# mLSTM in two chunks of 128 tokens in place of four chunks of 64

## The chip, the cores and the metric

The kernel runs on one core of a Trainium2 chip. The metric is the device time of one execution in microseconds, as the median of several runs. The engines are named as in the profile: PE (TensorE, products), PEld (its loads of weights), DVE (VectorE), ACT (ScalarE), POOL (GpSimd) and SP (SyncE, which issues the loads from memory).

## The reference

Two layers work on 256 tokens of width 1024. Each layer is a half-step FFN (SwiGLU), a mixer, and a second half-step FFN, with RMSNorm around each. The mixer projects its input, runs two groups of heads beside each other, differential attention and mLSTM, and projects both back. The change touches the mLSTM alone: 4 heads, keys of 64, values of 128. The reference works it in chunks of CHUNK = 64 tokens; shortened:

```
b = cumsum(log_f)                     # within a chunk
a = b_last - b + log_i
# the scan over chunks, state C (128 x 64), n (64), m:
m_new = max(bl + m, max(a));  w = exp(a - m_new);  decay = exp(bl + m - m_new)
C_new = decay * C + sum_l w_l v_l k_l^T;   n_new = decay * n + sum_l w_l k_l
# within a chunk, with the state from before it:
D = where(causal, b_j - b_s + log_i_s, -inf);  m = max(b + m_prev, max_s D)
w = exp(D - m) * (q k^T);  decay = exp(b + m_prev - m)
num = w v + decay * (q C_prev);  den = sum_s w + decay * (q n_prev)
h = num / max(|den|, exp(-m))
```

The chunk length does not change what h is, only how the sum over earlier tokens is split between the products within a chunk and the products with the state. The mask of the attention beside it has chunks of 64 of its own, and that stays.

## The kernel before

Weights arrive in pieces of 128 x 2048 (1 MB each). ACT makes of each half a rounded high part (wh, line 285), DVE the rest (wl, line 287), and every large product is three products on PE: wh with the high part of the input, wl with it, and wh with its low part (lines 335 to 337). These products are nearly all of PE's work.

In the mixer the projection runs over five groups of 512 columns, each for two tiles of 128 tokens (t = 0, 1). Its products are cut into 88 numbered steps. The small work of attention and mLSTM is cut into stages (`gate_chain`, `gate_decays`, `weighted_qk`, `scores`, `state`, `numerators` in `normed_ml`, `attend` and so on), and the table AT says ahead of which step each stage is issued. On PE the order of the program holds through the mixer. On the other engines a scheduler orders the instructions by its own estimates, and each engine then works its queue in that order.

PSUM holds a pool `bk` of four banks that the stages take in turn. A stage that takes a bank waits until the stage before it in that bank has been read out. Two banks `pin` hold the running projections; ACT or DVE empties one (`vd`, `vx`, `ra` and `rb`) before PE writes it again.

mLSTM with four chunks of 64, two per tile of tokens:
- `gate_chain` makes the running sums and maxima, starting again every 64 tokens (constants `scan`), and mp, the running maximum ahead of each chunk.
- `gate_decays` makes three rows of 256 exponents in ex: the factor of the state in a token's output, the weight of a token in the state, and the floor of the denominator. The first is rounded to eh.
- `weighted_qk` spreads eh over the rows with a product (L928), turns the other two rows round (L932), turns the keys round (L942), and makes qd (queries times the factor), dcy (the state's decay at the end of each chunk) and kwn (keys times their weights, for both tiles).
- `state(c)` for c = 0, 1, 2 makes the state after chunk c: four products of 64 x 64 weights on 129 columns, the last of which gathers the denominator (L1074), and an update of the state on DVE (L1078, L1081).
- `numerators(t)` sums into two banks: for each of the four heads a product within the tile (L1090, all 128 rows; the mask keeps the chunks apart), and behind it the product with the state: one on 64 rows for t = 0 (L1092, state after chunk 0) and two on 64 rows and 64 columns for t = 1 (L1095, states after chunks 1 and 2).
- `normed_ml` squares (ACT), takes the inverse root (POOL, rs), and scales (DVE, hn), which reads the two banks out.

fp32 products of the program make two records each in the trace.

Of the kernel before, what the change touches and what calls it, by code (L numbers as in the profile page):

```python
# [27 lines left out]
DFF = 2816  # L28
NC_FF = DFF // 256
KT = D // P  # L30
CH = 64
EPS = 1e-6
BIG = -1.0e30
DEFER = 3
AHEAD = 2
AT = (0, 2, 6, 6, 7, 22, 24, 24, 24, 24, 36, 31, 24, 38, 56, 34, 40, 40, 52, 57, 61, 60, 61, 67, 67, 67, 67, 71, 71, 78, 74, 74, 78, 84)
WARM = 6
SCRATCH = 1024
FILL = 896
# [82 lines left out]
class _Trunk:  # L122
# [49 lines left out]
    def constants_mix(self):  # L172
        nc, a = self.nc, self.a
# [3 lines left out]
        for name, shape in C1:  # L177
            n = math.prod(shape)
# [6 lines left out]
        for l in range(L):  # L185
# [27 lines left out]
                                     op=ALU.add)  # L213
# [7 lines left out]
        for t in range(NT):  # L221
            i = nc.scalar.activation(self.md[0:36, t], self.hot[0:36].unsqueeze(2).broadcast_to([36, 4, P]), AF.Copy)
# [5 lines left out]
        self.qd = self.ded.tile([P, 2, S], F32, name="qd")  # L228
# [426 lines left out]
class _Mixer:  # L655


    def __init__(self, tr, pre, l):
        self.tr, self.l = tr, l
        self.xT, self.r = pre  # L660
        self.yT = [[None, None] for _ in range(NT)]
        self.conved = None
        self.rot, self.qkT, self.so, self.C, self.p = [], [], [], [None], {}
# [204 lines left out]
    def gate_chain(self):  # L868
        tr, nc, stt, tt, ptg = self.tr, self.tr.nc, self.stt, self.tt, self.ptg
        gt = tr.t4("gt", (100, 4, S))  # L870
        bc, u, cm, M = (gt[:, i, :] for i in range(4))
# [10 lines left out]
        tt(self.c4(M), self.c4(cm), mp.unsqueeze(2).broadcast_to([100, 4, CH]), op=ALU.max)  # L882
# [23 lines left out]

    def gate_decays(self):

        tr, tt, c4 = self.tr, self.tt, self.c4
        bc, u, M = (v[0:36] for v in (self.bc, self.u, self.M))  # L910
        ex = self.ex = tr.t4("ex", (36, 3, S))
        tt(c4(ex[:, 0, :]), self.mp[0:36].unsqueeze(2).broadcast_to([36, 4, CH]), c4(M), op=ALU.subtract)
# [5 lines left out]
        tr.nc.vector.memset(ex[:, 0, 0:CH], 0.0)  # L918
        eh = self.eh = tr.t2("eh", (36, S), F32R)
        self.act(eh, ex[:, 0, :], AF.Copy)  # L920
        tt(eh[32:36], ex[32:36, 0, :], eh[32:36].bitcast(F32), op=ALU.subtract)

    def weighted_qk(self):

        tr, nc = self.tr, self.tr.nc
        pdb = tr.bank_bk((P, 2, S))
        for pr in range(2):
            self.mm(pdb[:, pr, :], tr.hotp[:, pr, :], self.eh, start=True, stop=True)  # L928
        ptn = tr.bank_bk((P, 2, NT, 4))
        for i in range(2):  # L930
            for t in range(NT):
                self.T(ptn[:, i, t, :], self.ex[0:4, 1 + i, t * P:(t + 1) * P], tr.ident[0:4, 0:4])  # L932
        self.wem = tr.small("wem", (P, 2, NT, 4))
# [5 lines left out]
        self.kwn = []  # L939
        for t in range(NT):  # L940
            for pr in range(2):
                self.T(ptk[:, t, pr, :], self.kT[:, pr, t * P:(t + 1) * P], tr.ident)  # L942
        for t in range(NT):
            kw = tr.t2("kwn", (P, 4, 64))
            self.tt(kw, ptk[:, t].rearrange("p a (h d) -> p (a h) d", h=2),
                    self.wem[:, 0, t, :].unsqueeze(2).broadcast_to([P, 4, 64]), op=ALU.mult)
            self.kwn.append(kw)
# [120 lines left out]
    def state(self, c):  # L1068
        tr, nc, mm, vx, C = self.tr, self.tr.nc, self.mm, self.tr.vx, self.C
        t, rows = c // 2, slice((c % 2) * 64, (c % 2) * 64 + 64)  # L1070
        pd = tr.bank_bk((P, 2, P + 1))
        for pr in range(2):
            for hh in range(2):
                mm(pd[hh * 64:hh * 64 + 64, pr, :], self.kwn[t][rows, 2 * pr + hh, :], vx[rows, t, 2 * pr + hh, :],  # L1074
                   start=True, stop=True)
        Cn = tr.small("C", (P, 2, P + 1), 3)
        if c == 0:
            nc.vector.tensor_copy(Cn, pd)  # L1078
        else:
            for pr in range(2):  # L1080
                self.stt(Cn[:, pr, :], C[c][:, pr, :], self.dcy[:, pr, c:c + 1], pd[:, pr, :], op0=ALU.mult, op1=ALU.add)  # L1081
        C.append(Cn)

    def numerators(self, t):
        tr, mm, vx, C = self.tr, self.mm, self.tr.vx, self.C
        num = [tr.bank_bk((P, 2, P + 1)) for _ in range(2)]
        for pr in range(2):
            for hh in range(2):
                rows, out = slice(hh * 64, hh * 64 + 64), num[hh][:, pr, :]
                mm(out, tr.wt[:, t, pr, hh, :], vx[:, t, 2 * pr + hh, :], start=True, stop=False)  # L1090
                if t == 0:
                    mm(out, tr.qd[rows, pr, 0:P], C[1][rows, pr, :], start=False, stop=True)  # L1092
                else:
                    for c in (2, 3):
                        mm(out[(c - 2) * 64:(c - 1) * 64], tr.qd[rows, pr, c * CH:(c + 1) * CH], C[c][rows, pr, :],  # L1095
                           start=False, stop=True)
# [13 lines left out]
    def normed_ml(self, t):  # L1110

        tr, act, tt = self.tr, self.act, self.tt
        num = self.numerators(t)
        ss = tr.small("ssm", (P, 4))
        dm = tr.small("dm", (P, 4))
        for h in range(4):
            act(tr.junk_tile(P), num[h % 2][:, h // 2, 0:P], AF.Square, scale=2.0 ** -3.5, accum_out=ss[:, h:h + 1])
        for hh in range(2):
            act(dm[:, hh::2], num[hh][:, :, P], AF.Abs)
        tt(dm, dm, self.wem[:, 1, t, :], op=ALU.max)  # L1120
        tt(dm, dm, dm, op=ALU.mult)
        self.stt(ss, dm, EPS, ss, op0=ALU.mult, op1=ALU.add)
        self.ts(ss, ss, 1e-37, 1e37, op0=ALU.max, op1=ALU.min)
# [50 lines left out]
```

## Time and profile before

| | before |
|---|---|
| median of 3 runs | 1004.95 us (1004.37 to 1006.48) |
| profiled execution | 1004.17 us |
| its span | 1002.4 us |
| mean granted TensorE clock | 0.996 |
| PE busy | 987.8 us, 99% of the span |
| DVE busy | 615.6 us, 61% |
| ACT busy | 523.6 us, 52% |
| POOL busy | 57.9 us, 6% |

The span runs from the first to the last instruction of the profiled execution; its own time is 1.77 us more. A row of the timeline gives the start, the time from start to end, the engine and line, what is written from what, the shape, the count, and in brackets the time that the engine stood idle before it and what ended that. Products overlap on PE, so the distance between two starts, not the duration, is what a product costs there. The mixer of the first layer lies about between 205 and 310 us, that of the second between 697 and 803 us.

### The profile page before, as it was taken

What the parts mean: (1) busy time and instruction counts of PE and PEld (TensorE: products, weight loads), DVE (VectorE), ACT (ScalarE), POOL (GpSimd) and SP (SyncE); (2) the same over time, 40 slices, a digit from 0 to 9 for tenths busy, and PEclk for the clock granted to TensorE, in tenths of its full rate; (3) what the DMA queues carried; (4) which work ended last, traced back from release to release, by engine and by line L of the source; (5) the groups of instructions that cost most, each with busy time, mean ns of one, the idle gap of its engine ahead of it and who ended that gap; (6) DMA issues with size and microseconds to landing.
All of it is one profiled execution on the core that took longest, in us unless ns stands there. A gap on an engine that the chain in (4) does not pass through costs nothing.

```text
span 1002.4 us, 12193 instructions
## 1 busy us (share of the span) xinstructions
PE 987.8 (99%) x4701; PEld 807.1 (81%) x4701; DVE 615.6 (61%) x867; ACT 523.6 (52%) x853; POOL 57.9 (6%) x59
## 2 busy tenths in 40 slices
PE   8999999999999999999999999999999999999997
PEld 5888888887788888888888888888877888888885
DVE  6755554589766755555485645456988586455542
ACT  6645444466755654445274544445768465454431
POOL 2000000014010000000000000001220100000000
PEclk9999999999999999999999999999999999999999
DMA  7954545335352745455346455543554247554511
GB/s 281 353 204 161 200 174 196 124 126 192 129 205 84 278 164 210 168 217 195 134 185 257 157 193 196 199 149 114 188 170 141 112 158 284 180 198 168 205 48 43
DMA packets 26809, 178.86 MB, mean 178 GB/s; under 512 B 2970, under 2 KB 3354, under 8 KB 6014
## 3 DMA queue, kind: packets, MB, share of 16 engines
q1 hardware_dynamic: 26750, 178.07, 48.5%
q8 instruction: 37, 0.61, 0.2%
q14 instruction: 22, 0.18, 0.1%
HBM read 177.01 MB, written 1.05 MB: 178 GB/s over the span
## 4 chain that ended last, share of the span: by engine, by line
PE 93%; DVE 4%; ACT 1%; DMA 1%; issue 0%; SPq 0%; DVEq 0%; POOLq 0%; ACTq 0%
PE pin L335 19%; PE pin L337 19%; PE pin L336 19%; PE bk L335 10%; PE bk L337 10%; PE bk L336 10%; PE ptr L466 2%; DVE wl L287 2%; DVE conv L810 1%; PE ptr L354 1%; ACT p L250 1%; PE ptr L778 1%; DMA wr<-in_w_dram 1%; PE bk L1090 1%; PE bk L1045 1%; ACT wh L285 0%
## 5 line engine op out<-in xcount | busy, mean ns | idle before, releaser
L287 DVE TENSOR_TENSOR wl<-wr,wh 128x1024 fp32r<-128x1024 f32 (+1 forms) x332 | 397.3, 1218 | 227.0 <-ACT wh L285 217.3
L285 ACT ACTIVATE wh<-wr 128x1024 fp32r<-128x1024 f32 (+1 forms) x332 | 340.5, 1045 | 203.0 <-PE pin L337 110.4
L335 PE MATMUL pin<-wh,th 128*128 128x512 f32 x880 | 349.2, 397 | 0.6 <-DVE rb L976 0.6
L337 PE MATMUL pin<-wh,tl 128*128 128x512 f32 x880 | 343.9, 391 | 0.0
L336 PE MATMUL pin<-wl,th 128*128 128x512 f32 x880 | 343.4, 390 | 0.0
L337 PEld LDWEIGHTS pin<-wh,tl 128*128 128x128 f32 x880 | 165.2, 188 | 35.0
L335 PEld LDWEIGHTS pin<-wh,th 128*128 128x128 f32 x880 | 165.3, 188 | 34.5 <-PE ptr L778 1.0
L336 PEld LDWEIGHTS pin<-wl,th 128*128 128x128 f32 x880 | 165.5, 188 | 32.4
L335 PE MATMUL bk<-wh,hh 128*128 128x512 f32 x352 | 140.0, 398 | 0.0
L337 PE MATMUL bk<-wh,hl 128*128 128x512 f32 x352 | 137.9, 393 | 0.0
L336 PE MATMUL bk<-wl,hh 128*128 128x512 f32 x352 | 137.6, 391 | 0.0
L469 ACT ACTIVATE hh<-ptr 128x256 fp32r<-128x256 f32 x88 | 33.2, 378 | 96.8 <-PE ptr L466 79.3
L250 ACT ACTIVATE sil<-pin,rs 128x256 f32<-128x256 f32 x86 | 40.6, 472 | 72.3 <-PE pin L337 69.0
L337 PEld LDWEIGHTS bk<-wh,hl 128*128 128x128 f32 x352 | 66.1, 188 | 13.7
L336 PEld LDWEIGHTS bk<-wl,hh 128*128 128x128 f32 x352 | 66.2, 188 | 12.7
L335 PEld LDWEIGHTS bk<-wh,hh 128*128 128x128 f32 x352 | 66.1, 188 | 12.8
L470 DVE TENSOR_TENSOR hl<-ptr,hh 128x256 fp32r<-128x256 f32 x88 | 37.0, 421 | 55.3 <-ACT hh L469 52.5
L343 POOL TENSOR_TENSOR rs<-s,c_half 128x1 f32<-128x1 f32 x24 | 18.0, 753 | 780.7 <-DVE s L383 771.4
L459 DVE SCALAR_TENSOR_TENSOR h<-pin,rs,sil 128x256 f32<-128x256 f32 x86 | 41.2, 479 | 30.3 <-ACT sil L250 30.3
L466 PEld LDWEIGHTS ptr<-c,h 128*128 128x128 f32 x176 | 24.7, 140 | 11.5
L400 DVE TENSOR_TENSOR tmp<-bk,gpost 128x512 f32<-128x512 f32 x24 | 16.3, 689 | 28.5 <-ACT junk L397 28.5
L466 PE MATMUL ptr<-c,h 128*128 128x128 f32 x176 | 33.4, 271 | 0.0
(169 smaller groups left out, 615.8 us busy)
## 6 DMA issues: line engine op xcount, KB each, us to landing
wr<-in_w_dram SPq DMA_DIRECT2D x162, 1024.0 KB, 4.8
gpost<-in_gpost_dram SPq DMA_DIRECT2D x6, 512.0 KB, 6.5
wr<-in_w_dram SPq DMA_DIRECT2D x3, 512.0 KB, 8.6
x<-in_x_dram SPq DMA_DIRECT2D x4, 256.0 KB, 7.0
out_dram<-x SPq DMA_DIRECT2D x4, 256.0 KB, 2.0
wr<-in_w_dram SPq DMA_DIRECT2D x2, 256.0 KB, 4.5
lamv<-in_lam_dram SPq DMA_DIRECT2D x1, 256.0 KB, 3.3
c<-in_c_dram SPq DMA_DIRECT2D x1, 222.0 KB, 6.7
```

What stands on the lines that cost most here:

```text
L250: i = self.nc.scalar.activation(*args, **kw)
L285: ia = nc.scalar.activation(hi[:, cs], raw[:, j, cs], AF.Copy)
L287: iv = nc.vector.tensor_tensor(lo[:, cs], raw[:, j, cs], hi[:, cs].bitcast(F32), op=ALU.subtract)
L335: mm(ps, xh, wh, start=start, stop=False)
L336: mm(ps, xh, wl, start=False, stop=False)
L337: mm(ps, xl, wh, start=False, stop=stop)
L343: self.nc.gpsimd.tensor_tensor(r, ss, self.half[:, :width], op=ALU.pow)
L400: nc.vector.tensor_tensor(tmp[hf], po[hf], g[:, hf * 512:hf * 512 + 512], op=ALU.mult)
L459: nc.vector.scalar_tensor_tensor(h, pin[:, 256:512], r, sil, op0=ALU.mult, op1=ALU.mult)
L466: nc.tensor.transpose(ptr[:, k, :], h[:, k * P:(k + 1) * P], self.ident)
L469: nc.scalar.activation(hh, ptr, AF.Copy)
L470: nc.vector.tensor_tensor(hl, ptr, hh.bitcast(F32), op=ALU.subtract)
```

## The change

The chunk length CH becomes 128, the length of a tile. There are two chunks, and the one state that is needed is that after the first tile. The first tile has no state before it, so its numerators have no product with a state at all. In the second tile the four products with the state stand behind all four products within the tile. The mask, the sums and maxima follow CH. ex has two rows in place of three (one row holds the weights of the first tile and the factors of the second), eh, qd and kwn are for one tile, dcy and the updates of the state go. AT loses two entries, those of two of the three `state` stages. The diff, with the helper c4 and signatures cut:

```diff
-CH = 64
+CH = P
@@ gate_chain
-        mp = self.mp = tr.small("mp", (100, 4))
+        mp = self.mp = tr.small("mp", (100, NT))
         nc.vector.memset(mp[:, 0:1], 0.0)
-        nc.vector.tensor_tensor_scan(mp[:, 1:4], self.c4(cm)[:, 0:3, CH - 1], self.c4(bc)[:, 0:3, CH - 1], 0.0,
-                                     op0=ALU.max, op1=ALU.add)
+        stt(mp[:, 1:2], cm[:, CH - 1:CH], 0.0, bc[:, CH - 1:CH], op0=ALU.max, op1=ALU.add)
...
@@ gate_decays
-        ex = self.ex = tr.t4("ex", (36, 3, S))
-        tt(c4(ex[:, 0, :]), self.mp[0:36].unsqueeze(2).broadcast_to([36, 4, CH]), c4(M), op=ALU.subtract)
-        tt(c4(ex[:, 1, :]), c4(u), c4(M)[:, :, CH - 1:CH].broadcast_to([36, 4, CH]), op=ALU.subtract)
-        self.stt(ex[:, 2, :], bc, -1.0, M, op0=ALU.mult, op1=ALU.subtract)
+        ex = self.ex = tr.t4("ex", (36, 2, S))
+        tt(ex[:, 0, 0:CH], u[:, 0:CH], M[:, CH - 1:CH].broadcast_to([36, CH]), op=ALU.subtract)
+        tt(ex[:, 0, CH:S], self.mp[0:36, 1:2].broadcast_to([36, CH]), M[:, CH:S], op=ALU.subtract)
+        self.stt(ex[:, 1, :], bc, -1.0, M, op0=ALU.mult, op1=ALU.subtract)
...
-        tr.nc.vector.memset(ex[:, 0, 0:CH], 0.0)
-        eh = self.eh = tr.t2("eh", (36, S), F32R)
-        self.act(eh, ex[:, 0, :], AF.Copy)
-        tt(eh[32:36], ex[32:36, 0, :], eh[32:36].bitcast(F32), op=ALU.subtract)
+        eh = self.eh = tr.t2("eh", (36, CH), F32R)
+        self.act(eh, ex[:, 0, CH:S], AF.Copy)
+        tt(eh[32:36], ex[32:36, 0, CH:S], eh[32:36].bitcast(F32), op=ALU.subtract)
@@ weighted_qk
-        pdb = tr.bank_bk((P, 2, S))
+        pdb = tr.bank_bk((P, 2, CH))
         for pr in range(2):
             self.mm(pdb[:, pr, :], tr.hotp[:, pr, :], self.eh, start=True, stop=True)
...
-        self.stt(tr.qd, self.q, 0.125, pdb, op0=ALU.mult, op1=ALU.mult)
-        self.dcy = tr.small("dcy", (P, 2, 4))
-        nc.vector.tensor_copy(self.dcy, pdb.rearrange("p a (c j) -> p a c j", c=4)[:, :, :, CH - 1])
-        ptk = tr.bank_bk((P, NT, 2, P))
...
+        self.stt(tr.qd, self.q[:, :, CH:S], 0.125, pdb, op0=ALU.mult, op1=ALU.mult)
+        ptk = tr.bank_bk((P, 2, P))
+        for pr in range(2):
+            self.T(ptk[:, pr, :], self.kT[:, pr, 0:P], tr.ident)
...
@@ state
+        pd = tr.bank_bk((P, 2, P + 1))
+        for pr in range(2):
+            for hh in range(2):
+                self.mm(pd[hh * 64:hh * 64 + 64, pr, :], self.kwn[:, 2 * pr + hh, :], tr.vx[:, 0, 2 * pr + hh, :],
+                        start=True, stop=True)
+        self.C = tr.small("C", (P, 2, P + 1))
+        tr.nc.vector.tensor_copy(self.C, pd)
@@ numerators
         for pr in range(2):
             for hh in range(2):
...
+                mm(num[hh][:, pr, :], tr.wt[:, t, pr, hh, :], tr.vx[:, t, 2 * pr + hh, :],
+                   start=pr == 0, stop=t == 0, skip_group_check=True)
+        if t:
+            for pr in range(2):
+                for hh in range(2):
+                    rows = slice(hh * 64, hh * 64 + 64)
+                    mm(num[hh][:, pr, :], tr.qd[rows, pr, :], self.C[rows, pr, :], start=False, stop=True,
+                       skip_group_check=True)
```

What it moves in the queues is seen at three places of the first layer. Lines shift by the edit: L1037 becomes L1022, L1052 L1037, L1055 L1040, L1127 L1108, L1120 to L1123 become L1101 to L1104. The first place is PE's queue at the state and the numerators of the first tile; L1037 (L1022) are transposes of attention that stand between. Before:

```order
L1074 MATMUL bk_2388<-vx,kwn_2155 64x129 x4
L1074 MATMUL bk_2395<-vx,kwn_2155 64x129 x4
L1037 MATMUL ptr_2406<-c_96,p_2339 128x128 x2
L1037 MATMUL ptr_2406<-c_96,p_2340 128x128 x2
L1090 MATMUL bk_2414<-vx,wt 128x129
L1092 MATMUL bk_2414<-C_2393,qd 128x129
L1090 MATMUL bk_2415<-vx,wt 128x129
L1092 MATMUL bk_2415<-C_2393,qd 128x129
```

With the change:

```order
L1059 MATMUL bk_2380<-vx,kwn_2149 64x129 x4
L1022 MATMUL ptr_2390<-c_96,p_2331 128x128 x2
L1022 MATMUL ptr_2390<-c_96,p_2332 128x128 x2
L1070 MATMUL bk_2398<-vx,wt 128x129
L1070 MATMUL bk_2399<-vx,wt 128x129
L1070 MATMUL bk_2398<-vx,wt 128x129
L1070 MATMUL bk_2399<-vx,wt 128x129
```

Before, four more rows like the last four follow, and twelve large products later a third L1074 x4; both are gone, and the products with the state between the others too. The second place is PE's queue at the numerators of the second tile. Before:

```order
L1090 MATMUL bk_2560<-vx,wt 128x129
L1095 MATMUL bk_2560<-C_2400,qd 64x129
L1095 MATMUL bk_2560<-C_2468,qd 64x129
L1090 MATMUL bk_2561<-vx,wt 128x129
L1095 MATMUL bk_2561<-C_2400,qd 64x129
L1095 MATMUL bk_2561<-C_2468,qd 64x129
```

and the same six once more. With the change these are all:

```order
L1070 MATMUL bk_2532<-vx,wt 128x129
L1070 MATMUL bk_2533<-vx,wt 128x129
L1070 MATMUL bk_2532<-vx,wt 128x129
L1070 MATMUL bk_2533<-vx,wt 128x129
L1076 MATMUL bk_2532<-C_2385,qd 128x129
L1076 MATMUL bk_2533<-C_2385,qd 128x129
L1076 MATMUL bk_2532<-C_2385,qd 128x129
L1076 MATMUL bk_2533<-C_2385,qd 128x129
```

The four products with the state now stand together behind the four within the tile. With two banks fewer taken by `state`, these two banks are now those that numerators(0) had taken. The third place is DVE's queue behind the first tile's denominators, where hn reads the first numerators out; ssa and y belong to `attend`. Before:

```order
L1123 TENSOR_SCALAR ssm_2424<-ssm_2424 128x4
L1127 TENSOR_TENSOR hn_2442<-bk_2414,rs_299_2440 128x2x128
L1127 TENSOR_TENSOR hn_2442<-bk_2415,rs_299_2440 128x2x128
L287 TENSOR_TENSOR wl_0_2663<-wr_2661,wh_0_2664 128x1024
L1052 SCALAR_TENSOR_TENSOR ssa_2503<-l_313_2512,ssa_2503 128x4
```

With the change:

```order
L1104 TENSOR_SCALAR ssm_2404<-ssm_2404 128x4
L287 TENSOR_TENSOR wl_0_2631<-wr_2629,wh_0_2632 128x1024
L1037 SCALAR_TENSOR_TENSOR ssa_2475<-l_307_2484,ssa_2475 128x4
L1108 TENSOR_TENSOR hn_2422<-bk_2398,rs_295_2420 128x2x128
L1108 TENSOR_TENSOR hn_2422<-bk_2399,rs_295_2420 128x2x128
L1040 TENSOR_TENSOR y_2489<-bk_2470,rs_308_2487 128x512
```

hn now stands behind a cast of weights and behind ssa. The queues of POOL and SP keep their order, and ACT's changes only behind the squares of `attend`, where two casts of weights now come after all eight squares.

More of the change, by code (lines that the diff above doesn't have):

```diff
@@ L35 @@
 AHEAD = 2
-AT = (0, 2, 6, 6, 7, 22, 24, 24, 24, 24, 36, 31, 24, 38, 56, 34, 40, 40, 52, 57, 61, 60, 61, 67, 67, 67, 67, 71, 71, 78, 74, 74, 78, 84)
+AT = (0, 2, 6, 6, 7, 22, 24, 24, 24, 24, 36, 31, 24, 38, 56, 34, 40, 40, 52, 57, 61, 60, 61, 67, 67, 67, 71, 78, 74, 74, 78, 84)
 WARM = 6
@@ L227, in constants_mix @@
         self.qk = self.ded.tile([P, 4, S], F32, name="qk")
-        self.qd = self.ded.tile([P, 2, S], F32, name="qd")
+        self.qd = self.ded.tile([P, 2, CH], F32, name="qd")
         self.vx = self.ded.tile([P, NT, 4, P + 1], F32, name="vx")
@@ L662, in __init__ @@
         self.conved = None
-        self.rot, self.qkT, self.so, self.C, self.p = [], [], [], [None], {}
+        self.rot, self.qkT, self.so, self.p = [], [], [], {}
         self.aT, self.lsum, self.hn, self.y = [None] * NT, [None] * NT, [None] * NT, [None] * NT
@@ L751, in stages @@
             lambda: self.scores(1, 2),
-            lambda: self.state(0),
-            lambda: self.state(1),
+            self.state,
             lambda: self.combine(1, 0),
             lambda: self.normed_ml(0),
-            lambda: self.state(2),
             lambda: self.combine(1, 2),
@@ L876, in gate_chain @@
         nc.vector.tensor_tensor_scan(cm, tr.scan[:, 1, :], u, 0.0, op0=ALU.add, op1=ALU.max)
-        mp = self.mp = tr.small("mp", (100, 4))
+        mp = self.mp = tr.small("mp", (100, NT))
         nc.vector.memset(mp[:, 0:1], 0.0)
-        nc.vector.tensor_tensor_scan(mp[:, 1:4], self.c4(cm)[:, 0:3, CH - 1], self.c4(bc)[:, 0:3, CH - 1], 0.0,
-                                     op0=ALU.max, op1=ALU.add)
-        tt(self.c4(M), self.c4(cm), mp.unsqueeze(2).broadcast_to([100, 4, CH]), op=ALU.max)
+        stt(mp[:, 1:2], cm[:, CH - 1:CH], 0.0, bc[:, CH - 1:CH], op0=ALU.max, op1=ALU.add)
+        tt(M.rearrange("p (c j) -> p c j", c=NT), cm.rearrange("p (c j) -> p c j", c=NT),
+           mp.unsqueeze(2).broadcast_to([100, NT, CH]), op=ALU.max)
         mh = tr.t2("mh", (100, S), F32R)
@@ L907, in gate_decays @@
     def gate_decays(self):
-        tr, tt, c4 = self.tr, self.tt, self.c4
+        tr, tt = self.tr, self.tt
         bc, u, M = (v[0:36] for v in (self.bc, self.u, self.M))
-        ex = self.ex = tr.t4("ex", (36, 3, S))
-        tt(c4(ex[:, 0, :]), self.mp[0:36].unsqueeze(2).broadcast_to([36, 4, CH]), c4(M), op=ALU.subtract)
-        tt(c4(ex[:, 1, :]), c4(u), c4(M)[:, :, CH - 1:CH].broadcast_to([36, 4, CH]), op=ALU.subtract)
-        self.stt(ex[:, 2, :], bc, -1.0, M, op0=ALU.mult, op1=ALU.subtract)
+        ex = self.ex = tr.t4("ex", (36, 2, S))
@@ L923, in weighted_qk @@
+        self.act(eh, ex[:, 0, CH:S], AF.Copy)
+        tt(eh[32:36], ex[32:36, 0, CH:S], eh[32:36].bitcast(F32), op=ALU.subtract)
     def weighted_qk(self):
         tr, nc = self.tr, self.tr.nc
-        pdb = tr.bank_bk((P, 2, S))
+        pdb = tr.bank_bk((P, 2, CH))
         for pr in range(2):
             self.mm(pdb[:, pr, :], tr.hotp[:, pr, :], self.eh, start=True, stop=True)
[L929 to L932, printed above, removed]
@@ L933, in weighted_qk @@
-        self.wem = tr.small("wem", (P, 2, NT, 4))
-        nc.vector.tensor_copy(self.wem, ptn)
-        self.stt(tr.qd, self.q, 0.125, pdb, op0=ALU.mult, op1=ALU.mult)
-        self.dcy = tr.small("dcy", (P, 2, 4))
-        nc.vector.tensor_copy(self.dcy, pdb.rearrange("p a (c j) -> p a c j", c=4)[:, :, :, CH - 1])
-        ptk = tr.bank_bk((P, NT, 2, P))
[L939 to L947, printed above, removed]
+        ptn = tr.bank_bk((P, 1 + NT, 4))
+        for n, row in enumerate((self.ex[0:4, 0, 0:P], self.ex[0:4, 1, 0:P], self.ex[0:4, 1, P:S])):
+            self.T(ptn[:, n, :], row, tr.ident[0:4, 0:4])
+        self.wem = tr.small("wem", (P, 1 + NT, 4))
@@ L949, in intra_weights @@
+        nc.vector.tensor_copy(self.wem, ptn)
+        self.stt(tr.qd, self.q[:, :, CH:S], 0.125, pdb, op0=ALU.mult, op1=ALU.mult)
+        ptk = tr.bank_bk((P, 2, P))
+        for pr in range(2):
+            self.T(ptk[:, pr, :], self.kT[:, pr, 0:P], tr.ident)
+        self.kwn = tr.t2("kwn", (P, 4, 64))
+        self.tt(self.kwn, ptk.rearrange("p a (h d) -> p (a h) d", h=2),
+                self.wem[:, 0, :].unsqueeze(2).broadcast_to([P, 4, 64]), op=ALU.mult)
     def intra_weights(self):
@@ L1066, in values_ml, with state @@
                                             AF.Copy, scale=self.r[t])
-    def state(self, c):
-        tr, nc, mm, vx, C = self.tr, self.tr.nc, self.mm, self.tr.vx, self.C
-        t, rows = c // 2, slice((c % 2) * 64, (c % 2) * 64 + 64)
+    def state(self):
+        tr = self.tr
         pd = tr.bank_bk((P, 2, P + 1))
@@ L1073, in state @@
             for hh in range(2):
[L1074 to L1082, printed above, removed]
+                self.mm(pd[hh * 64:hh * 64 + 64, pr, :], self.kwn[:, 2 * pr + hh, :], tr.vx[:, 0, 2 * pr + hh, :],
+                        start=True, stop=True)
+        self.C = tr.small("C", (P, 2, P + 1))
+        tr.nc.vector.tensor_copy(self.C, pd)
     def numerators(self, t):
-        tr, mm, vx, C = self.tr, self.mm, self.tr.vx, self.C
+        tr, mm = self.tr, self.mm
         num = [tr.bank_bk((P, 2, P + 1)) for _ in range(2)]
@@ L1088, in numerators @@
             for hh in range(2):
[L1089 to L1096, printed above, removed]
+                mm(num[hh][:, pr, :], tr.wt[:, t, pr, hh, :], tr.vx[:, t, 2 * pr + hh, :],
[6 more added lines that the diff above has]
+                       skip_group_check=True)
         return num
@@ L1119, in normed_ml @@
             act(dm[:, hh::2], num[hh][:, :, P], AF.Abs)
-        tt(dm, dm, self.wem[:, 1, t, :], op=ALU.max)
+        tt(dm, dm, self.wem[:, 1 + t, :], op=ALU.max)
         tt(dm, dm, dm, op=ALU.mult)
```

3 lines of the change are left out of this document (removed).

## The prediction

> **What bounds the kernel now.** I read the page first: which engine is busy, and whose work the chain of waits runs through.
>
> ```profile
> span 1002.4 us, 12193 instructions
> PE 987.8 (99%) x4701; PEld 807.1 (81%) x4701; DVE 615.6 (61%) x867; ACT 523.6 (52%) x853; POOL 57.9 (6%) x59
> ...
> PE 93%; DVE 4%; ACT 1%; DMA 1%; issue 0%; SPq 0%; DVEq 0%; POOLq 0%; ACTq 0%
> ...
> L287 DVE TENSOR_TENSOR wl<-wr,wh 128x1024 fp32r<-128x1024 f32 (+1 forms) x332 | 397.3, 1218 | 227.0 <-ACT wh L285 217.3
> ```
>
> TensorE is busy for 99% of the span and carries 93% of the chain. Work taken off its queue shortens the run, unless what stands next in the queue is not ready. Its waits in the mixer, for both layers together:
>
> ```profile
> PE bk L928 <- DVE eh L921: 1.5, 2, 0.7
> PE bk L1092 <- DVE C L1078: 0.4, 2, 0.2
> ...
> ACT wh L285 <- DMA wr<-in_w_dram: 19.7, 16, 3.1
> ```
>
> Each count of 2 is once per layer. The layers run alike, so I work out the first and double it. The profiled run took 1004.17 us, 1.77 us beyond its span and 0.78 us under the median of the runs, 1004.95.
>
> **Term A, weights of queries and keys.** TensorE's timeline (start, busy, line, operands, count, idle before):
>
> ```profile
> 242.69 0.50 PE L928 MATMUL bk<-eh,c_hotp 36*128 36x256 f32 x2 [0.74 <-DVE eh L921]
> 243.12 0.41 PE L932 MATMUL bk<-c,ex 4*128 4x4 f32 x4
> 243.46 0.66 PE L942 MATMUL bk<-c,qk 128*128 128x128 f32 x4
> 243.95 0.60 PE L778 MATMUL ptr<-c,ra 128*128 128x128 f32 x4
> 244.35 0.47 PE L335 MATMUL pin<-wh,th 128*128 128x512 f32 x1
> ```
>
> The change halves the columns of L928, drops one of four L932 (0.34/4 = 0.09) and two of four transposes of L942 (0.49/2 = 0.25). The halved columns save between nothing and half of the 0.43 that L928 takes to the next row; I take 0.1, since loading the array is not halved. That is 0.43 us of TensorE, but TensorE waits here for VectorE before and behind:
>
> ```profile
> 230.50 0.41 DVE L912 TENSOR_TENSOR ex<-mp,gt 36x256 f32<-36x256 f32 x1
> 235.11 0.11 DVE L918 MEMSET ex<- 36x64 f32 x1
> 235.15 0.41 DVE L810 SCALAR_TENSOR_TENSOR conv<-xpad,c,conv 128x256 f32<-128x256 f32 x1
> 242.22 0.41 DVE L921 TENSOR_TENSOR eh<-ex,eh 4x256 fp32r<-4x256 f32 x1
> 243.34 0.87 DVE L976 SCALAR_TENSOR_TENSOR rb<-pin,rs,c 128x256 f32<-128x256 f32 x2
> ```
>
> eh ends at 242.63 and L928 starts 0.06 later; rb ends at 244.21 and the pin product starts 0.14 later, since it writes the bank that rb empties. So this stage ends with VectorE's chain. A column there costs (1.218 - 0.41)/768 = 1.05 ns, by the wl row of 1024 columns and L912 of 256. L912 and L913 lose 128 columns each (0.27), the memset goes (0.04 to the next row), eh loses 128 columns (0.13): 0.44 us earlier. Bounds: 0.13 if only eh's own cut counts, 0.87 if rb does not gate and TensorE's 0.43 comes on top. I take **0.44**. What qd, dcy and the second kwn save on VectorE I cost at nothing: TensorE has products to do behind them. GpSimd's ra, which holds TensorE until 237.1 (229.60 + 7.50, a row below), ends before this chain and is left as it is. ScalarE and the work behind follow TensorE here, so their times move with A.
>
> **Term B, state and first numerators.** TensorE again:
>
> ```profile
> 268.62 0.68 PE L1074 MATMUL bk<-vx,kwn 64*64 64x129 f32 x16
> 269.23 0.66 PE L1037 MATMUL ptr<-c,p 128*128 128x128 f32 x4
> 269.73 0.39 PE L1090 MATMUL bk<-vx,wt 128*128 128x129 f32 x2
> 270.33 0.49 PE L1092 MATMUL bk<-C,qd 64*128 64x129 f32 x2 [0.22 <-DVE C L1078]
> 270.75 0.49 PE L1090 MATMUL bk<-vx,wt 128*128 128x129 f32 x2
> ...
> 273.25 0.50 PE L335 MATMUL pin<-wh,th 128*128 128x512 f32 x1
> ...
> 276.20 0.66 PE L1074 MATMUL bk<-vx,kwn 64*64 64x129 f32 x8
> 276.79 0.66 PE L1037 MATMUL ptr<-c,p 128*128 128x128 f32 x4
> ...
> 277.98 0.39 PE L335 MATMUL pin<-wh,th 128*128 128x512 f32 x1
> ...
> 279.34 2.84 PE L1045 MATMUL bk<-vd,aT 128*128 128x128 f32 x24
> 281.93 0.48 PE L335 MATMUL pin<-wh,th 128*128 128x512 f32 x1
> ```
>
> A product of the program makes two records. The twelve of attend (L1045), all 128x128, take (281.93 - 279.34)/12 = 0.216 us each. The eight of numerators(0) take 0.42 each, by the starts 270.33 and 270.75: L1090 on 128 rows alternates with L1092 on 64 rows, and each change costs 0.20 more than a product behind one of its own shape. [...]
>
> Four products of L1090's shape are left, one behind the other: 4 x 0.216 = 0.86 in place of 273.25 - 269.73 = 3.52, so 2.66. The wait for C, 0.22 of it, goes because C is first read in numerators(1), some 12 us later. At worst they stay at 0.42 (1.68, saving 1.84). State: four products, on 128 rows and 64 columns, replace 0.61 (eight in four quarters) and 0.59 (four in two quarters, 276.20 to 276.79). The new shape is not in the trace. If column halves run side by side as in the x8 row it is 0.59, if not 4 x 0.216 = 0.86; I take 0.59, as there too only the column halves differ. So 0.61. Together 3.27, between 2.2 and 3.3.
>
> Who is late next? ScalarE:
>
> ```profile
> 268.58 1.28 ACT L244 ACT_TABLE_LOAD   x1
> ...
> 274.29 0.70 ACT L990 ACTIVATE vd<-pin,rs 128x512 f32<-128x512 f32 x1
> ...
> 277.48 0.60 ACT L1038 ACTIVATE aT<-ptr 128x512 f32<-128x512 f32 x1 [0.91 <-PE ptr L1037]
> ```
>
> Between the first two rows ScalarE is not idle, so vd is not ready before 274.99 however early its product ends. The product at 277.98 overwrites the bank that vd empties; it would be up at 277.98 - 3.27 = 274.71 and waits to 275.05. That gives back **0.34** (nothing if ScalarE is early too). The aT behind it has 0.91 of idle time to give: it can end near 276.57 + 0.60 = 277.2, and its first reader, eight products into attend, comes at 276.4 + 1.73 = 278.1. B is 3.27 - 0.34 = **2.93**.
>
> **Term C, second numerators.**
>
> ```profile
> 284.76 0.39 PE L1090 MATMUL bk<-vx,wt 128*128 128x129 f32 x2
> ...
> 287.80 0.66 PE L778 MATMUL ptr<-c,y 128*128 128x128 f32 x4
> ...
> 292.44 0.60 PE L778 MATMUL ptr<-c,y 128*128 128x128 f32 x4
> ...
> 252.70 1.16 PE L1005 MATMUL bk<-qkT,qkT 64*128 64x128 f32 x16
> 253.79 0.50 PE L335 MATMUL pin<-wh,th 128*128 128x512 f32 x1
> ```
>
> Now 3.04 us with a change of shape at every step. Then four of L1070 (0.86), one change (0.20), four of L1076 on alternating row halves into two banks. L1005 does eight like that in 1.09, so four take 0.55 (at worst 0.86, one by one). Sum 1.61, C = **1.43**, between 1.1 and 1.6.
>
> C's cover: num(1) now takes the two banks of num(0), whose reader hn has moved behind ssa on VectorE.
>
> ```profile
> 278.53 1.02 POOL L343 TENSOR_TENSOR rs<-ssm,c_half 128x4 f32<-128x4 f32 x1 [32.04 <-DVE ssm L1123]
> 279.59 0.76 DVE L1127 TENSOR_TENSOR hn<-bk,rs 128x256 f32<-128x256 f32 x2 [1.20 <-POOL rs L343]
> 281.77 0.15 DVE L1052 SCALAR_TENSOR_TENSOR ssa<-l,ssa 128x4 f32<-128x4 f32 x1
> ...
> 229.60 7.50 POOL L977 TENSOR_TENSOR ra<-ra,rb 128x512 f32<-128x512 f32 x1 [5.67 <-DVE rb L976]
> ```
>
> ssa stands 2.43 behind the start of attend (279.34). With attend at 276.4 and ScalarE some 0.5 behind, ssa comes near 279.4 and hn ends near 280.2. num(1) is up at 284.76 - 2.93 = 281.8: no wait, 1.6 us to spare.
>
> **Sum.** 0.44 + 2.93 + 1.43 = 4.80 per layer, 9.6 for two; 1004.17 - 9.6 = 994.6 for the profiled run, 995.3 from the median. Nothing outside the mixer is changed, and no DMA is added; TensorE's chain has no other wait on which the gain could stop.
>
> **Rivals.**
> 1. ScalarE is the bound in this stretch: casts, squares and vd come a further 1 to 2 us late per layer. For it: no idle time from 268.58 to vd. Against: 0.91 idle right behind. Gain 2.8 to 3.8 per layer: 997.4 to 999.4 (rivals are counted from the median).
> 2. L1070 stays at 0.42, because of its 129 columns or its weights and not the change of shape. B loses 0.82, C 0.62 (1.68 in place of 0.86 + 0.20), and the wait for vd, 0.34, goes: gain 3.7 per layer, 997.6. Against: L1045, weights of the same form with 128 columns, at 0.216.
> 3. The gain is given back: TensorE comes 9.6 us earlier to weights that are no earlier. For it: casts waited 19.7 us for DMA in 16 waits. Against: none of these waits reached TensorE. If the weights set the pace, the time stays near 1004.
> 4. Slower: GpSimd's rs, one step of 1.02 for each of hn, the first y and the second y, slows down beside VectorE as its ra did, which took 7.50. The first step begins near 278.0; VectorE's queue has the first ssa, hn, first y, second ssa, second y in this order, so the second y ends three steps and some 1.6 us of VectorE later. TensorE begins to wait for hn once a step takes over 2.6. It is slower than before once the second y ends after 292.9 (its transposes stood at 292.44, and A has moved the clock by 0.44), that is from 4.4 a step. At 7.50 it ends at 302.1, 9.2 too late per layer: 1023. For it: hn now stands behind a cast and ssa. Against: the step took 1.02 with casts beside it.
>
> **How the numbers follow.** Forecast 0.70, ScalarE 0.15, pitch 0.09, given back 0.03, slower 0.03. The forecast's own bounds are A 0.13 to 0.87, B 1.9 to 3.3, C 1.1 to 1.6: 3.1 to 5.8 per layer, all at once being unlikely; the range 993.0 to 999.0 leaves out the worst sums and the upper part of rival 1. Faster by over 0.2% (2 us, about what a measurement of this kernel can tell from no change) 0.94, within it 0.03, slower 0.03.
>
> **What would show it.** L1070 at 0.22 per product and numerators(0) under 1 us; numerators(1) near 1.6; state near 0.6 once per layer; the wait of L928 near 0.3; a new wait of some 0.3 for vd. Wrong would be: L1070 starts 0.42 apart, TensorE waiting for hn, y or aT, or waits for casts behind the mixer.

## The result, and the profile after

The changed kernel takes 995.26 us (median of 4 runs, 995.03 to 995.47). The kernel before, run beside it, takes 1005.61 us (median of 4, 1004.37 to 1006.48). The ratio is 0.9897, with a 95% interval of 0.9886 to 0.9909: faster by 10.35 us, where 9.6 were forecast, and inside the range of 993.0 to 999.0 us.

The page of the changed kernel, busy time by engine and the shares of the chain of waits:

```profile
span 993.2 us, 12033 instructions
PE 978.4 (99%) x4631; PEld 801.9 (81%) x4631; DVE 609.3 (61%) x853; ACT 522.5 (53%) x853; POOL 61.1 (6%) x59
...
PE 94%; POOL 2%; ACT 1%; DVE 1%; DMA 1%; issue 0%; SPq 0%; DVEq 0%; POOLq 0%; ACTq 0%
```

PE lost 9.4 us of busy time (987.8 to 978.4) and 70 records, and is still busy 99% of the span. What it waited for in the mixers of the changed kernel (total for both layers, times, longest):

```profile
PE ptr L776 <- POOL ra L962: 1.2, 2, 0.6
...
PE pin L335 <- ACT vd L975: 0.7, 2, 0.4
```

The waits for eh and for C are gone. The wait for vd is the one that term B foresaw. The wait for ra, GpSimd's rotation, was there before too, with 0.9 in all, and so was a wait for rb of 0.6.

PE's timeline of the changed kernel at the weights of queries and keys, and GpSimd's and VectorE's work ahead of it. The answers to the prediction's rows under term A:

```profile
238.80 0.66 PE L776 MATMUL ptr<-c,ra 128*128 128x128 f32 x4 [0.62 <-POOL ra L962]
...
243.52 0.44 PE L920 MATMUL bk<-eh,c_hotp 36*128 36x128 f32 x2
...
244.79 0.48 PE L335 MATMUL pin<-wh,th 128*128 128x512 f32 x1
...
231.13 7.62 POOL L962 TENSOR_TENSOR ra<-ra,rb 128x512 f32<-128x512 f32 x1 [5.66 <-DVE rb L961]
...
232.78 4.82 DVE L808 SCALAR_TENSOR_TENSOR conv<-xpad,c,conv 128x256 f32<-128x256 f32 x12
...
241.35 1.28 DVE L913 TENSOR_TENSOR eh<-ex,eh 4x128 fp32r<-4x128 f32 x1
```

I count from the start of GpSimd's ra, which both kernels reach in the same way. To the pin product it was 244.35 - 229.60 = 14.75 us, and is 244.79 - 231.13 = 13.66: **1.09** a layer, where A said 0.44.

PE's timeline at the state, the numerators of the first tile, attend and the numerators of the second:

```profile
269.06 0.66 PE L1059 MATMUL bk<-vx,kwn 128*64 128x129 f32 x8
269.65 0.66 PE L1022 MATMUL ptr<-c,p 128*128 128x128 f32 x4
270.14 1.06 PE L1070 MATMUL bk<-vx,wt 128*128 128x129 f32 x8
270.96 0.47 PE L335 MATMUL pin<-wh,th 128*128 128x512 f32 x1
...
273.81 0.60 PE L1022 MATMUL ptr<-c,p 128*128 128x128 f32 x4
...
275.47 0.50 PE L335 MATMUL pin<-wh,th 128*128 128x512 f32 x1 [0.37 <-ACT vd L975]
...
276.97 2.84 PE L1030 MATMUL bk<-vd,aT 128*128 128x128 f32 x24
...
282.38 1.06 PE L1070 MATMUL bk<-vx,wt 128*128 128x129 f32 x8
283.37 0.71 PE L1076 MATMUL bk<-C,qd 64*128 64x129 f32 x8
284.02 0.66 PE L776 MATMUL ptr<-c,y 128*128 128x128 f32 x4
...
279.70 0.74 DVE L1108 TENSOR_TENSOR hn<-bk,rs 128x256 f32<-128x256 f32 x2
```

The last row is VectorE's. From the state to attend it was 279.34 - 268.62 = 10.72, and is 7.91: **2.81**. From attend to behind the second numerators it was 287.80 - 279.34 = 8.46, and is 7.05: **1.41**. hn ends at 280.44, 1.9 us before its banks are wanted at 282.38, and there is no wait for it.

The sum is 1.09 + 2.81 + 1.41 = 5.31 a layer, 10.6 for two. From the start of ra to the end of the span it was 1002.4 - 229.60 = 772.8, and is 993.2 - 231.13 = 762.1, a difference of 10.7. The spans differ by only 9.2, since the profiled execution of the changed kernel started later. The first load of weights in the chain of waits (start, time to landing), before and then after:

```profile
2.10 5.89 DMA wr<-in_w_dram
```

```profile
2.09 7.45 DMA wr<-in_w_dram
```

That is 1.56 us, about the 1.53 us by which ra starts later. The change touches nothing there, and three profiles of the changed kernel had 5.39, 7.16 and 7.45. So kernels are compared below by pieces of their traces as well as by medians.

### The profile page after: what moved, and what is told of

Its sections match the earlier page's. It is cut to its first block, busy times and chain, and to the rows that moved or that the text cites. A ratio compares the mean times of both kernels' runs of the same rounds, so it can differ in the third digit from the quotient of the medians.

```text
span 993.2 us, 12033 instructions
## 1 busy us (share of the span) xinstructions
PE 978.4 (99%) x4631; PEld 801.9 (81%) x4631; DVE 609.3 (61%) x853; ACT 522.5 (53%) x853; POOL 61.1 (6%) x59
## 4 chain that ended last, share of the span: by engine, by line
PE 94%; POOL 2%; ACT 1%; DVE 1%; DMA 1%; issue 0%; SPq 0%; DVEq 0%; POOLq 0%; ACTq 0%
PE pin L335 19%; PE pin L337 19%; PE pin L336 19%; PE bk L335 10%; PE bk L337 10%; PE bk L336 10%; PE ptr L466 2%; POOL ra L962 2%; PE ptr L354 1%; ACT wh L285 1%; PE ptr L776 1%; DMA wr<-in_w_dram 1%; PE bk L990 1%; DVE wl L287 1%; PE bk L1030 1%; ACT vd L975 0%
## 5 line engine op out<-in xcount | busy, mean ns | idle before, releaser
L343 POOL TENSOR_TENSOR rs<-s,c_half 128x1 f32<-128x1 f32 x24 | 18.0, 752 | 781.0 <-DVE s L383 771.8
```

Source lines behind the costliest of these rows:

```text
L343: self.nc.gpsimd.tensor_tensor(r, ss, self.half[:, :width], op=ALU.pow)
```

## The experiments

**1. The order of the products alone.** The kernel before keeps its four chunks of 64, and only puts the products within the tile ahead of those with the state:

```diff
         for pr in range(2):
             for hh in range(2):
+                mm(num[hh][:, pr, :], tr.wt[:, t, pr, hh, :], vx[:, t, 2 * pr + hh, :], start=pr == 0, stop=False,
+                   skip_group_check=True)
+        for pr in range(2):
+            for hh in range(2):
                 rows, out = slice(hh * 64, hh * 64 + 64), num[hh][:, pr, :]
-                mm(out, tr.wt[:, t, pr, hh, :], vx[:, t, 2 * pr + hh, :], start=True, stop=False)
...
```

> The kernel before with its four chunks of 64, but in each tile all four products within the tile first and the products with the states behind them. If changes of the array's shape cost 0.20 each (the prediction): numerators(0) takes 0.86 + 0.20 + 0.55 = 1.6 us in place of 3.5, numerators(1) 0.86 + 0.20 + 0.6 = 1.7 in place of 3.0, 3.3 per layer, 6.6 in all, near 999. If 0.42 belongs to the products' own form (rival 2): both stay at 3.0 to 3.5 and the time near 1005.6.

Measured: 1000.26 us against 1006.11 of the kernel before, a ratio of 0.9943 (0.9928 to 0.9957). PE's timeline of this kernel:

```profile
271.01 1.06 PE L1089 MATMUL bk<-vx,wt 128*128 128x129 f32 x8
272.00 0.72 PE L1095 MATMUL bk<-C,qd 64*128 64x129 f32 x8
272.65 0.50 PE L335 MATMUL pin<-wh,th 128*128 128x512 f32 x1
...
284.17 1.06 PE L1089 MATMUL bk<-vx,wt 128*128 128x129 f32 x8
285.16 0.67 PE L1098 MATMUL bk<-C,qd 64*64 64x129 f32 x16
286.69 0.66 PE L778 MATMUL ptr<-c,y 128*128 128x128 f32 x4 [0.86 <-DVE y L1055]
```

The numerators of the first tile take 272.65 - 271.01 = 1.64 us in place of 3.52, with the same eight products of the program. Those of the second take 286.69 - 0.86 - 284.17 = 1.66 in place of 3.04; then PE waits 0.86 for y, and 0.36 in the second layer, which takes back 1.2 of the 6.5 us that the two layers save there. No operation is removed here, so what goes is a cost of the order, and the rival that the products with 129 columns are slow in themselves falls. The order changes two things, though: the shape stays the same from product to product, and a product no longer stands right behind the one that sums into the same columns. Experiment 2 tells these apart. By the medians the gain is 5.85 of the change's 10.35 us; by the traces, from the start of ra to the end of the span, it is 772.8 - (998.3 - 230.88) = 5.4 of 10.7. So about half of the change is the order alone.

**2. The same cost, put back.** In the changed kernel, the product with the state follows each head's product within the tile again, in the second tile:

```diff
-        if t:
-            for pr in range(2):
-                for hh in range(2):
+                if t:
                     rows = slice(hh * 64, hh * 64 + 64)
                     mm(num[hh][:, pr, :], tr.qd[rows, pr, :], self.C[rows, pr, :], start=False, stop=True,
```

The changed kernel, unaltered, ran beside it, and for that this was expected:

> The changed kernel once more, as the measure for the runs beside it: 995 to 996 us, the same waits (0.6 for ra, 0.3 for rb, 0.36 for vd in each layer), and a start that differs by the time of the first weights' landing.

and for the alternating order:

> The changed kernel, but in the second tile each product with the state stands right behind its head's product within the tile. If changes of shape cost 0.20 each: numerators(1) takes 8 x 0.42 = 3.4 us in place of 1.64, 1.7 per layer, 3.5 in all, near 999. If halving the states alone made the gain: 1.64 stays and the time is that of the changed kernel.

Measured: 994.04 us (992.92 to 995.73) for the changed kernel, under the 995 to 996 expected, and 998.45 us (997.75 to 998.96) for the alternating one, 4.4 more. PE's timeline of the alternating kernel:

```profile
282.05 0.39 PE L1070 MATMUL bk<-vx,wt 128*128 128x129 f32 x2
282.37 0.49 PE L1074 MATMUL bk<-C,qd 64*128 64x129 f32 x2
282.79 0.49 PE L1070 MATMUL bk<-vx,wt 128*128 128x129 f32 x2
283.21 0.49 PE L1074 MATMUL bk<-C,qd 64*128 64x129 f32 x2
...
285.29 0.66 PE L776 MATMUL ptr<-c,y 128*128 128x128 f32 x4
```

Each step but the first (0.32) is 0.42 again, and the numerators take 285.29 - 282.05 = 3.24 where the changed kernel's grouped ones take 1.64. That is 1.60 a layer, 3.2 for two. From 282.79 to 283.21 the next product sums into the same columns, from 282.37 to 282.79 it goes to the other bank. Both take 0.42, so it is the change of shape that costs, and not the sum into the same columns. From the start of ra to the end of the span it is 996.0 - 230.80 = 765.2 against 991.1 - 229.11 = 762.0, the same 3.2; the two profiles differ by another 1.7 ahead of ra, where the edit changes nothing. The two experiments agree, with 1.60 / 6 = 0.27 us for each of the six changes of shape that the alternating order adds here, and (3.52 - 0.22 - 1.64) / 6 = 0.28 for each of the six that the grouped order takes out of the first tile's numerators in experiment 1 (0.22 is the wait for C). What TensorE does at such a change was not shown.

**3. The memset that the change removes.** A was too small, and the largest row under it that the prediction had priced at next to nothing is this memset (0.04 us to the next row). VectorE and GpSimd before, in the same stretch:

```profile
231.51 3.64 DVE L810 SCALAR_TENSOR_TENSOR conv<-xpad,c,conv 128x256 f32<-128x256 f32 x9
235.11 0.11 DVE L918 MEMSET ex<- 36x64 f32 x1
...
235.88 1.50 DVE L810 SCALAR_TENSOR_TENSOR conv<-xpad,c,conv 128x256 f32<-128x256 f32 x1
...
222.20 1.73 POOL L977 TENSOR_TENSOR ra<-ra,rb 128x512 f32<-128x512 f32 x1 [9.71 <-DVE rb L976]
```

Twelve convolution instructions surround the memset. Eleven follow each other by about 0.40 us; the last takes 1.50. In the changed kernel all twelve take 4.82 together. GpSimd's ra, 1.73 at its shortest in this layer, takes 7.50 beside them, and 7.62 in the changed kernel. The theory, drawn from these rows alone: the memset lets GpSimd's ra in, and one convolution then waits for it. First, the kernel before without the memset; the exponent of the first chunk is made so small instead (through a copy mz of mp with a start of -1e30) that the factor comes out as zero:

```diff
+        mz = self.mz = tr.small("mz", (36, 4))
+        nc.vector.memset(mz[:, 0:1], BIG)
+        nc.vector.tensor_copy(mz[:, 1:4], mp[0:36, 1:4])
-        tt(c4(ex[:, 0, :]), self.mp[0:36].unsqueeze(2).broadcast_to([36, 4, CH]), c4(M), op=ALU.subtract)
+        tt(c4(ex[:, 0, :]), self.mz.unsqueeze(2).broadcast_to([36, 4, CH]), c4(M), op=ALU.subtract)
-        tr.nc.vector.memset(ex[:, 0, 0:CH], 0.0)
```

> The kernel before without the memset between the convolutions on VectorE: the first chunk's factor becomes zero through a starting maximum of -1e30, in a small tile filled far ahead. Opening theory (the memset let GpSimd's sum ra in, and a convolution then waited for it): the twelve convolutions take 4.8 us in place of 5.9, L928 no longer waits for eh (0.74 before), some 0.7 per layer, 1.3 in all. The prediction's price: the memset cost 0.04, the convolutions stay at 5.8, L928 waits 0.7, the time is the same.

Measured: 1005.07 us against 1006.11, a ratio of 0.9989 (0.9979 to 0.9999). PE, VectorE and GpSimd of this kernel:

```profile
239.64 0.66 PE L778 MATMUL ptr<-c,ra 128*128 128x128 f32 x4 [0.86 <-POOL ra L979]
...
244.36 0.50 PE L930 MATMUL bk<-eh,c_hotp 36*128 36x256 f32 x2
...
245.97 0.48 PE L335 MATMUL pin<-wh,th 128*128 128x512 f32 x1
...
231.69 7.89 POOL L979 TENSOR_TENSOR ra<-ra,rb 128x512 f32<-128x512 f32 x1 [5.67 <-DVE rb L978]
```

From the start of ra to the product with eh it took 242.69 - 229.60 = 13.09 before, and 12.67 here; to the pin product it took 14.75 before, and 14.28 here: 0.42 and 0.47 a layer. From ra to the end of the span it is 1003.5 - 231.69 = 771.8 against 772.8. The wait for eh is gone (no bracket at L930), and the wait for ra has grown from 0.47 to 0.86. So eh comes 1.1 us earlier behind ra (11.90 in place of 13.03), of which 0.47 reached PE: it had waited only 0.74 for eh, and the next wait took about half of that.

Then the memset is put into the changed kernel, on 36 x 64 numbers that nothing reads, at three places among the twelve convolutions: behind the ninth, where it was, behind the second, and behind the sixth. The diff is that for the ninth, shortened by the lines that collect the convolutions in convs. The one for the sixth names convs[4]; the one for the second waits for done alone.

```diff
-        ex = self.ex = tr.t4("ex", (36, 2, S))
+        ex3 = tr.t4("ex", (36, 3, S))
+        ex = self.ex = ex3[:, 0:2, :]
...
+        tr.after(tr.nc.vector.memset(ex3[:, 2, 0:64], 0.0), [done, self.convs[5]])
```

> The changed kernel with a memset of 36x64 that nobody reads put back between the ninth and the tenth convolution, where it stood before. Opening theory: one convolution behind it takes about 1.5 in place of 0.4, the twelve some 5.9 in place of 4.8, and the product of eh waits again, 0.2 to 0.5 per layer. The prediction's price: 0.04 longer, no wait for eh.

> The same memset between the second and the third convolution. Opening theory: GpSimd gets in some 2 to 3 us earlier, its sum takes about 4.5 us in place of 7.6, the transposes' wait for it (0.62) goes, a convolution near the fourth takes 1.5, and the convolutions end 1.1 later. If openings do not matter: the sum takes 7.6 and the wait stays at 0.62.

> The changed kernel with a memset of 36 x 64 numbers that nothing reads, now behind the sixth of the twelve convolution instructions (behind the second it let nothing in, behind the ninth it did). If GpSimd can enter from some time after its rotation was issued (2.5 us is too early, 5.3 us is enough), the sixth lies between at about 4.1 us: one convolution then takes 1.5 us or more, the rotation on GpSimd ends early and the twelve take 5.9 us, with the time near 997 us; or they keep their 4.85 us and the rotation its 7.6 us, with the time near 994.8 us. Either halves the stretch in which the limit can lie.

Measured, one time each: 996.85, 994.79 and 995.60 us. VectorE and GpSimd with the memset behind the ninth:

```profile
236.96 0.11 DVE L913 MEMSET ex<- 36x64 f32 x1
...
237.32 1.52 DVE L809 SCALAR_TENSOR_TENSOR conv<-xpad,c,conv 128x256 f32<-128x256 f32 x1
...
231.71 6.85 POOL L965 TENSOR_TENSOR ra<-ra,rb 128x512 f32<-128x512 f32 x1 [5.67 <-DVE rb L964]
...
244.31 0.44 PE L923 MATMUL bk<-eh,c_hotp 36*128 36x128 f32 x2 [0.49 <-DVE eh L916]
...
245.97 0.47 PE L335 MATMUL pin<-wh,th 128*128 128x512 f32 x1
```

behind the second:

```profile
233.43 3.98 DVE L808 SCALAR_TENSOR_TENSOR conv<-xpad,c,conv 128x256 f32<-128x256 f32 x10
...
230.93 7.63 POOL L964 TENSOR_TENSOR ra<-ra,rb 128x512 f32<-128x512 f32 x1 [5.67 <-DVE rb L963]
```

and behind the sixth:

```profile
234.63 0.11 DVE L913 MEMSET ex<- 36x64 f32 x1
...
236.19 1.50 DVE L809 SCALAR_TENSOR_TENSOR conv<-xpad,c,conv 128x256 f32<-128x256 f32 x1
...
230.57 6.85 POOL L965 TENSOR_TENSOR ra<-ra,rb 128x512 f32<-128x512 f32 x1 [5.66 <-DVE rb L964]
```

Behind the ninth and the sixth the memset brings the long convolution and the wait for eh back (0.49 and 0.47). Up to the product with eh that costs PE (244.31 - 231.71) - (243.52 - 231.13) = 0.21 a layer. But rb comes later with it, and holds the pin product again: that starts 245.97 - 231.71 = 14.26 behind ra (14.25 with the memset behind the sixth), in place of 13.66. So the memset costs **0.60** a layer. The traces as a whole agree: from the start of ra to the end of the span they take 763.3 and 763.2 us against the 762.0 of the changed kernel, 1.2 for two layers. Behind the second the memset does nothing: the next ten take 3.98, 0.40 each, ra its 7.63, and from ra to the end it is 762.1. So not every memset between convolutions shortens ra. It is also not the instruction behind the memset that is long. It is the eleventh in both, which starts 5.61 and 5.62 us after ra did; before, it was the twelfth, 6.28 us after ra (235.88 - 229.60). What decides between these, and why a memset 2.5 us behind the start of ra does nothing and one 4.1 us behind it does, was not found.

**4. The two waits that are left.** Both can be shifted in the table AT. A higher entry means that its stage is issued behind more of the large products. The diff with both entries raised:

```diff
-AT = (0, 2, 6, 6, 7, 22, 24, 24, 24, 24, 36, 31, 24, 38, 56, 34, 40, 40, 52, 57, 61, 60, 61, 67, 67, 67, 71, 78, 74, 74, 78, 84)
+AT = (0, 2, 6, 6, 7, 22, 24, 24, 24, 24, 36, 31, 24, 38, 56, 36, 40, 40, 52, 57, 61, 60, 61, 67, 67, 70, 71, 78, 74, 74, 78, 84)
```

The first is the transposes of ra (the wait for ra), the second `normed_ml` of the first tile, whose numerators and squares stand ahead of vd (the wait for vd). Each alone, beside the changed kernel's 994.04:

> The changed kernel with one entry of AT moved: the transposes that wait for GpSimd's ra (0.62 per layer) come two steps, 1.4 us, later in TensorE's queue. If this wait is TensorE's own loss: it goes, the next wait (rb) takes some 0.2 of it, 0.4 per layer, 0.8 in all. If the work behind is bound by VectorE's chain to eh anyway: eh or rb are waited for instead and the time stays.

> The changed kernel with one entry of AT moved: the first numerators and their squares three steps later, so that ScalarE makes vd before two of the squares. If ScalarE's queue makes the wait for vd (0.36 per layer), it goes and 0.7 in all is gained. If the wait belongs to the product that vd empties, it stays.

Measured: 994.67 (993.13 to 994.83) and 993.32 us (992.21 to 994.55). Each took its own wait off PE's list. The medians alone say nothing of the first; the start of the executions varies by more than the 0.8 us expected of it (the first load took 5.39 to 7.45 us in profiles of the changed kernel). Hence both together, beside the changed kernel:

> The changed kernel with two entries of the table AT raised: roped(0, 1) from 34 to 36 and normed_ml(0) from 67 to 70. Inside the traces each entry alone gained: the piece from the first rotated product to the state products took 37.45 us against 37.88 (0.43 a layer), and from the state products to the end of the span 723.54 us against 724.10 (0.56 for both layers). If these gains are real and add up, the two together give 2 x 0.43 + 0.56 = 1.4 us: about 1.4 us under the changed kernel of the same job. If the waits only pass to the next instruction that would have waited, the two kernels agree within 0.5 us.

> The changed kernel, unaltered, beside the version with both entries raised. Its time should lie between 993.5 and 995.7 us, where its earlier medians lie (995.26 and 994.04); its span minus the landing of the first weights on the chain should again be 985.7 us, as in both its traces (993.2 - 7.45 and 991.1 - 5.39), if the start alone makes its executions differ.

Measured: 993.46 us (992.33 to 994.48), a ratio of 0.9880 (0.9863 to 0.9897) to the kernel before, and 995.21 us (993.27 to 995.74), 0.9892 (0.9874 to 0.9910), for the changed kernel. GpSimd's ra and the state's first product, with both entries raised:

```profile
232.07 7.63 POOL L962 TENSOR_TENSOR ra<-ra,rb 128x512 f32<-128x512 f32 x1 [5.67 <-DVE rb L961]
...
269.56 0.66 PE L1059 MATMUL bk<-vx,kwn 128*64 128x129 f32 x8
```

and in the changed kernel beside it:

```profile
231.40 7.62 POOL L962 TENSOR_TENSOR ra<-ra,rb 128x512 f32<-128x512 f32 x1 [5.67 <-DVE rb L961]
...
269.31 0.66 PE L1059 MATMUL bk<-vx,kwn 128*64 128x129 f32 x8
```

From ra to the state it is 37.49 against 37.91. From there to the end of the span (992.7 and 993.4) it is 723.1 against 724.1. So 1.4 us are gained by the traces, as expected. The medians differ by 1.75, with ranges that overlap. By the trace the kernel with both is the fastest here, by a little; its median and that of the second entry alone (993.32) are the same within their ranges. The changed kernel's span less its first load is 993.4 - 7.16 = 986.2, not the 985.7 expected, so the first load is not all that varies ahead of the mixer; from ra to the end it is 762.0, 762.0 and 762.1 us in its three profiles.

## Why the prediction was right

**Right in the time and in two of three terms.** Per layer:

| term | predicted | measured |
|---|---|---|
| A, weights of queries and keys | 0.44 (0.13 to 0.87) | 1.09 |
| B, state and first numerators | 2.93 (1.9 to 3.3) | 2.81 |
| C, second numerators | 1.43 (1.1 to 1.6) | 1.41 |
| sum | 4.80 | 5.31 |

**B.** The numerators of the first tile take 270.96 - 270.14 = 0.82 (0.86 predicted), the state 0.59 once (0.59), both as priced. ScalarE's vd came when the sum said: the product that waits for it starts 275.47 - 269.06 = 6.41 behind the state, where 275.05 - 268.62 = 6.43 was forecast. But the wait costs more than the 0.34 of the sum. This product starts 0.75 behind the one ahead (at 274.72) and the next one 0.34 behind it, where these products otherwise start 0.23 apart: 0.63. The 0.37 in the bracket counts only from the end of the product ahead, and these products overlap. Some 0.2 us of that had been won ahead of the wait, where PE was earlier than forecast by as much (from 270.96 to 273.81 it took 2.85 where 273.25 to 276.20 had been 2.95; the rest is 0.04 in the numerators and 0.05 behind the transposes). What PE saves ahead of vd, the wait for vd takes.

**C.** 284.02 - 282.38 = 1.64, predicted 1.61. The banks were free in time: hn had 1.9 us to spare, 1.6 predicted.

**A is the step that failed**, beyond its upper bound, with 1.09 for 0.44. "The memset goes (0.04 to the next row)" priced the memset by its own row. The row to look at was the convolution two rows on, which took 1.50 where its neighbours take 0.40. Experiment 3 shows what that is worth: with the memset back behind the ninth convolution, A would be 14.75 - 14.26 = 0.49, near the 0.44 chosen, with eh and rb as the gates that the prediction names. The memset is the other 0.60.

It reaches PE in two parts. PE no longer waits for eh, where the prediction still saw some 0.3; it waits for ra (0.62), which the prediction left as it is. That is the 0.21 up to L920. And rb no longer holds the pin product, so that PE's own saving counts: from L920 to there it takes 1.27 in place of 1.66, 0.39, which the upper bound had held and the chosen value had not. So "this stage ends with VectorE's chain" holds only while that chain is the late one.

What the memset is worth depends on what stands beside it. Taken out of the kernel before, it gives 0.47: there ra is waited for longer (0.86), and PE has all its products. One more item of A came out otherwise: eh, counted 0.13 shorter, takes 1.28 in place of 0.41, beside GpSimd's next ra (239.22 to 242.48). It ends at 242.63, 0.89 before PE's product, and costs nothing.

**The rivals.** ScalarE as the bound: it costs the 0.63 at vd and no more; PE's list for the mixers has no other wait for it. Products that stay at 0.42: four of L1070 take 0.82, and experiment 1 shows the same. A gain given back to late weights: PE has no wait for a cast behind the mixer. A slow rs: it did not occur; its first step took 1.02 us as before, and hn was on time.

The median was met to 0.04 us, which is luck: the 0.5 a layer that the sum lacked is 1.0 us for two, about as much as medians of the same kernel differ from one set of runs to the next (994.04, 995.21, 995.26).

## What to carry to other kernels

Before pricing an instruction that goes, look at the next few rows for one that is longer than its neighbours: what the instruction does to its neighbours can be many times its own duration (here 0.60 us a layer for a memset of 0.11). Group small products by shape: the order alone was worth about half of this change (5.85 of 10.35 us by the medians), without removing any work. When a stage waits for two engines in turn, work out what gates it once the first wait is gone; here VectorE's chain came 1.1 us earlier without the memset, and PE gained 0.5 to 0.6 of it, since it then waited for GpSimd.

## What was not expected of the hardware

**GpSimd beside VectorE.** In the first layer ra takes 1.73 us at its shortest, and 6.85 to 7.89 beside the convolutions. Even the shortest is not undisturbed. Two of VectorE's rows in the kernel before, and one of GpSimd's:

```profile
222.69 1.78 DVE L887 SCALAR_TENSOR_TENSOR md<-mh,c_hot 36x512 fp32r<-36x512 f32 x1
...
239.88 2.31 DVE L287 TENSOR_TENSOR wl<-wr,wh 128x1024 fp32r<-128x1024 f32 x1
...
238.99 2.12 POOL L977 TENSOR_TENSOR ra<-ra,rb 128x512 f32<-128x512 f32 x1 [1.89 <-DVE rb L976]
```

The first ra (222.20, 1.73) is issued while the first of two md instructions runs; that ends at 222.78, ra 1.15 later, and the second md takes 1.78 where the first took 0.69. The ra of 238.99 is issued during a cast that ends at 239.95; ra ends 1.16 later, and the next cast takes 2.31 in place of about 1.2. With a memset behind the sixth or ninth convolution ra ends at 6.85, which is 1.24 after the long convolution starts (5.61); in the kernel before at 7.50, 1.22 after (6.28). With no long convolution it ends at 7.62, 1.15 after the last of the twelve (232.78 + 4.82 - 231.13 = 6.47). So by these rows ra needs some 1.2 us once it gets in, and GpSimd stands still through nearly the whole row of convolutions (both are an estimate from the ends of VectorE's instructions), although ra was issued 1.65 us before the first of them. (The profile's times of GpSimd are rough.)

Where a VectorE instruction is long in these rows, it is so by about what ra is estimated to need: a convolution takes 1.50 in place of 0.40 us, md 1.78 in place of 0.69, the cast 2.31 in place of about 1.2. The instruction that already runs when ra is issued, 0.11 to 0.24 us into it, is never the long one. The order of issue alone does not decide which of the two engines waits: ra was issued ahead of all twelve convolutions, and by the estimate got in behind ten of them (with a memset behind the sixth or ninth), eleven (before) or twelve (changed kernel). What the two engines contend for, no run shows. Why ra gets in behind the cast of 238.75, and not behind the one that ran when the long ra was issued, was not found.

**The start.** The first load of weights took 5.39 to 7.45 us from issue to landing in three profiled executions of the changed kernel. That is a spread of 2.1 us, more than the 1.4 that the two raised entries are worth.
